# Gate tiles among the merges, merge sums on VectorE, earlier splits of pooled features, recurrence gates one tile later

## The chip, the core and the metric

The kernel runs on one core of a Trainium2 chip. The metric is the device time of one execution in microseconds (us). The core's engines run side by side and wait for each other through semaphores: PE is TensorE's matmul, PEld its weight load, DVE is VectorE, ACT is ScalarE, POOL is GpSimd, SP only issues DMAs. "Clock" is the clock that TensorE was granted as a share of full speed (1.00 is 2.4 GHz, 0.50 is 1.2 GHz).

## What is computed

Two transformer-like models run one after the other on 256 tokens of width 1024, in fp32. Only what the change touches is written out here.

```python
# first block, once
h = rms_norm(x); qa,ka,va,qc,kc,vc,rx,rgate,gates = split(h @ w_in)
ya = moba_attention(qa, ka, va)
xr = causal_dwconv(rx)                          # 4 taps
r = sigmoid(xr @ w_a + b_a); i = sigmoid(xr @ w_x + b_x)   # block-diagonal, 64 wide
yb = scan(exp(-8 r softplus(-lam)), r, i, xr) * gelu(rgate)
yc = rms_norm(diff_attention(qc, kc, vc))
g  = sigmoid(gates + b_gate)                    # 3 x 1024 columns
x  = x + (g0*(ya @ w_branch_a) + g1*(yb @ w_branch_b) + g2*(yc @ w_branch_c)) @ w_out
x  = x + (gelu(conv(rms_norm(x) @ up_g)) * conv(rms_norm(x) @ up_v)) @ ffn_down
x  = rms_norm(x)
# second block, two layers
u,q,k,v,xc,gate_b,gate_c,gate_logits = split(x @ w_in)
oa = (windowed_mean(u) - u) @ w_pool * pool_scale
ob = sliding_window_attention(rope(q), rope(k), v)
oc = gate_b * conv(gate_c * xc)
g  = sigmoid(gate_logits)
x  = layer_norm(a*x + (g0*(oa @ w_branch_a) + g1*(ob @ w_branch_b) + g2*(oc @ w_branch_c)) @ w_o)
x  = layer_norm(a*x + (silu(conv(x @ up_a)) * conv(x @ up_b)) @ w_down)
```

## The kernel before

Everything is held transposed: features on the 128 partitions, the 256 tokens along a row. An fp32 product is made of three matmuls over numbers that are split into a high and a low part: high times high (L332), high weight times low data (L333), low weight times high data (L334). One 128x128 weight tile thus gives three matmuls of 256 columns, and an output tile with eight such weight tiles gives 24.

All weights lie packed in HBM in the order in which they are used. The class `Stream` loads them in chunks of eight tiles (512 KB), and each chunk is split once: ACT copies the high part (`whi`, L175), DVE subtracts for the low part (`wlo`, L176). There are six raw buffers and five pairs of `whi` and `wlo`; `begin` issues the splits of the next chunks a little ahead of the tile that needs them. Each engine works its queue in order; the order comes from a scheduler over the written program.

`phase` runs a list of output tiles: the matmuls of one, its evacuation, and then one step (`fill.slot`) of each attention generator that is live, so that attention work lies between weight tiles. `fill.add` queues generators, `fill.drain` runs them to their end. `reg(i)` hands out one of nine large buffers R0 to R8, `wrk()` one of 13 temporaries of 128x256, `ps()` one of eight PSUM buffers. `split` writes a value's high part with ACT (L344) and its low part with DVE (L345).

The places that the change touches:

- **Recurrence gates.** In the first block tiles of RX and of gate 0 alternate. RX's evacuation is a convolution (L664, L666) and a split into `wrk`; `rg_front(m)` multiplies that split by two block-diagonal weights (6 matmuls) and works out the recurrence's coefficients. `rg_front(m-1)` comes after the gate tile of m, with three tiles between it and its RX tile; `rg_front(7)` comes after the first QC tile, with two. `rg_back` does the scan on DVE.
- **Differential attention's norm.** `diff_norm` turns the four heads' results into `yc` by a reciprocal root on ACT (L460, another activation table than the gates' L763) and a chain on DVE with a split. Three gate tiles follow it, then `rope_tables` (DVE work for the second block, L718 to L731) and the merges.
- **Merges.** One for each of eight output tiles m: three products over the branches (16 weight tiles in the first block, 8 in a layer), each evacuated by DVE with its gate (L859), then two sums and a split into `mg`. Up to m = 5 the sums (L863, L864) and the low part (L872) are POOL's and the high part (L867) and a scaled copy (L871) are ACT's; for m = 6 and 7 the sums and the low part (L869) are DVE's. `late` and `settle` put the split behind the next merge's products. The projection w_out or w_o reads `mg` next, in `seam`: its first three output tiles take k = 0 to 5 of all three first, and k = 6 and 7 after that.
- **Pooled features.** In a layer, two POOL2 tiles are evacuated by a chain of windowed sums (`pool_evac`), and `pool_mix`, after four gate tiles, first splits the two results (L344, L345) and then multiplies them (6 matmuls).

Of the kernel before, what the change touches and what calls it, by code (L numbers as in the profile page):

```python
# [22 lines left out]
NWIN = 6  # L23
POOLAT = 4
# [37 lines left out]
def _plan():  # L62
# [10 lines left out]
    for m in range(8):  # L73
        cols("w_in", 0, RX + m * P)
        cols("w_in", 0, GT + m * P)
        if m:
            runs.append(("rg", 0, 2, m - 1, 1))
    for c in (QC, KC):
        for m in range(4):
            cols("w_in", 0, c + m * P)  # L80
            if c == QC and m == 0:
                runs.append(("rg", 0, 2, 7, 1))
# [3 lines left out]
    for m in range(8, 24):  # L86
        cols("w_in", 0, GT + m * P)
    for m in range(8):
        cols("w_branch_a", 0, m * P, 4)
        cols("w_branch_b", 0, m * P, 8)  # L90
        cols("w_branch_c", 0, m * P, 4)
# [7 lines left out]
    for l in range(2):  # L99
# [10 lines left out]
        for m in range(24):  # L110
            if m == POOLAT:
                runs.append(("pool2", l, 2, 0, 1))
            cols("w_in_2", l, GT2 + m * P)
        for m in range(8):
            cols("w_branch_a_2", l, m * P, 2)
            cols("w_branch_b_2", l, m * P, 4)
            cols("w_branch_c_2", l, m * P, 2)
# [107 lines left out]
def _build(tc, ctx, ap):  # L225
# [549 lines left out]
    for m in range(8):  # L775
        phase([dict(t0=AT["w_in", 0, RX + m * P], nk=8, rhs=HX, evac=rx_evac(m)), gm[m]])
        if m:
            phase([rg_front(m - 1)])
# [61 lines left out]
    phase(gm[:5])  # L840
# [3 lines left out]
    phase(gm[5:])  # L844
    mg = (reg(1, F32R), reg(7, F32R))

    def merge(l, names, nks, srcs, mg):
        def go(m):
# [17 lines left out]
            def parts():  # L866
# [305 lines left out]
```

## Time and profile before

| | |
|---|---|
| median of three runs | 1225.6 us (1219.65 to 1226.5) |
| the profiled execution's own time | 1220.18 us |
| its span, first to last instruction | 1218.4 us |
| mean granted clock | 0.985 |
| PE, DVE, ACT, POOL busy | 1173.7, 948.7, 772.8, 306.7 us |

Busy time counts an engine as busy while an instruction is in flight; matmuls overlap, so PE's busy time hides how far apart they start. The idle time of PE, and the stretches in which matmuls start further apart than elsewhere, are what the rows below are read for.

### The profile page before, as it was taken

How to read it: one execution, taken by the hardware profiler on the slowest of the kernel's cores; microseconds unless marked ns; L12 is line 12 of the kernel's file. 1: busy time of each engine (PE TensorE's matmuls, PEld its weight loads, DVE VectorE, ACT ScalarE, POOL GpSimd, SP SyncE). 2: the span in 40 equal slices, each digit the busy share in tenths (PEclk: the TensorE clock that was granted, in tenths of full speed). 3: DMA queues.
4: the chain of work that ended last, by engine and by line, in shares of the span. 5: the costliest groups of instructions: out<-in, count | busy, mean ns of one | idle time of the engine just before them, and what ended most of it. 6: DMA issues, size and time to landing. Idle time of an engine off the chain costs nothing.

```text
span 1218.4 us, 25304 instructions
## 1 busy us (share of the span) xinstructions
PE 1173.7 (96%) x9928; PEld 1154.2 (95%) x9928; DVE 948.7 (78%) x1713; ACT 772.8 (63%) x1411; POOL 306.7 (25%) x287
## 2 busy tenths in 40 slices
PE   8999999999999999989998999999999998999995
PEld 8998999998999999989998999999999997999995
DVE  7988886788988856876579888757986688987754
ACT  7678566846766645666456766645776556765642
POOL 2033120141132210121155322122320263222122
PEclk9999999999999999989999999999999998999998
DMA  7654545466466655544544466655544553465641
GB/s 285 225 160 138 189 139 175 127 195 202 157 211 196 205 198 179 182 148 156 173 147 152 155 221 196 215 184 170 166 164 158 184 178 124 159 203 184 200 145 35
DMA packets 60487, 212.62 MB, mean 175 GB/s; under 512 B 6864, under 2 KB 9296, under 8 KB 60368
## 3 DMA queue, kind: packets, MB, share of 16 engines
q1 hardware_dynamic: 60080, 210.88, 53.0%
q8 instruction: 77, 1.26, 0.4%
q14 instruction: 42, 0.34, 0.1%
q10 hardware_dynamic: 288, 0.14, 0.1%
HBM read 209.94 MB, written 1.05 MB: 173 GB/s over the span
## 4 chain that ended last, share of the span: by engine, by line
PE 63%; DVE 18%; ACT 8%; POOL 5%; issue 5%; DMA 0%; POOLq 0%; SPq 0%; ACTq 0%; DVEq 0%
PE ps L333 20%; PE ps L332 20%; PE ps L334 20%; DVE wlo L176 7%; ACT whi L175 4%; POOL wrk L925 2%; DVE R L499 1%; POOL wrk L864 1%; DVE wrk L919 1%; DVE wrk L918 1%; PE ps L552 1%; PE ps L749 1%; PE ps L582 1%; PE ps L748 1%; PE ps L750 1%
## 5 line engine op out<-in xcount | busy, mean ns | idle before, releaser
L176 DVE TENSOR_TENSOR wlo<-raw,whi 128x1024 fp32r<-128x1024 f32 (+1 forms) x401 | 501.4, 1254 | 141.6 <-ACT whi L175 136.2
L332 PE MATMUL ps<-hh,whi 128*128 128x256 f32 x1912 | 538.3, 282 | 4.0 <-ACT hh L450 4.0
L333 PE MATMUL ps<-hl,whi 128*128 128x256 f32 x1912 | 534.0, 280 | 3.3 <-DVE hl L451 3.1
L334 PE MATMUL ps<-hh,wlo 128*128 128x256 f32 x1912 | 533.0, 279 | 0.6 <-DVE wlo L176 0.4
L175 ACT CAST whi<-raw 128x1024 fp32r<-128x1024 f32 (+1 forms) x401 | 413.5, 1037 | 149.3 <-PE ps L333 107.4
L332 PEld LDWEIGHTS ps<-hh,whi 128*128 128x128 f32 x1912 | 362.1, 190 | 7.3 <-ACT hh L450 4.6
L333 PEld LDWEIGHTS ps<-hl,whi 128*128 128x128 f32 x1912 | 364.2, 191 | 4.5 <-DVE hl L451 4.0
L334 PEld LDWEIGHTS ps<-hh,wlo 128*128 128x128 f32 x1912 | 362.1, 190 | 1.0 <-DVE wlo L176 1.0
L332 PE MATMUL ps<-R,whi 128*128 128x256 f32 (+1 forms) x1176 | 329.9, 281 | 5.2 <-ACT whi L175 1.9
L333 PE MATMUL ps<-R,whi 128*128 128x256 f32 (+1 forms) x1176 | 329.6, 280 | 5.3 <-DVE R L499 3.0
L334 PE MATMUL ps<-R,wlo 128*128 128x256 f32 (+1 forms) x1176 | 328.5, 279 | 2.6 <-DVE wlo L176 2.6
L333 PEld LDWEIGHTS ps<-R,whi 128*128 128x128 f32 x1176 | 222.6, 189 | 7.8 <-DVE R L499 4.4
L332 PEld LDWEIGHTS ps<-R,whi 128*128 128x128 f32 x1176 | 222.9, 190 | 6.9 <-ACT R L867 2.3
L334 PEld LDWEIGHTS ps<-R,wlo 128*128 128x128 f32 x1176 | 222.5, 189 | 3.4 <-DVE wlo L176 3.4
L925 POOL TENSOR_TENSOR wrk<-wrk 128x256 f32<-128x256 f32 x63 | 82.8, 1315 | 239.7 <-DVE wrk L919 150.3
L344 ACT CAST R<-wrk 128x256 fp32r<-128x256 f32 x89 | 36.0, 407 | 109.5 <-POOL wrk L925 95.2
L918 DVE SCALAR_TENSOR_TENSOR wrk<-ps,par,wrk 128x255 f32<-128x255 f32 x120 | 56.7, 477 | 17.3 <-ACT wrk L917 17.3
L600 POOL TENSOR_SCALAR a_lg<-a_lg,a_r 128x256 f32<-128x256 f32 x24 | 28.8, 1198 | 131.7 <-DVE a_r L575 77.9
L394 POOL TENSOR_TENSOR n_sq<-n_sq,n_q 128x256 f32<-128x256 f32 x42 | 39.6, 942 | 82.4 <-ACT n_q L385 81.2
L345 DVE TENSOR_TENSOR R<-wrk,R 128x256 fp32r<-128x256 f32 x89 | 39.6, 447 | 26.4 <-ACT R L344 26.2
L919 DVE SCALAR_TENSOR_TENSOR wrk<-ps,par,wrk 128x254 f32<-128x254 f32 x120 | 57.2, 477 | 1.6
L863 POOL TENSOR_TENSOR wrk<-wrk 128x256 f32<-128x256 f32 x18 | 17.3, 960 | 137.6 <-DVE wrk L859 137.4
(231 smaller groups left out, 1153.5 us busy)
## 6 DMA issues: line engine op xcount, KB each, us to landing
raw<-in_wst SPq DMA_DIRECT2D x395, 512.0 KB, 3.7
x<-in_xT SPq DMA_DIRECT2D x4, 256.0 KB, 5.1
out_y<-x SPq DMA_DIRECT2D x3, 256.0 KB, 2.2
cst<-in_cst SPq DMA_DIRECT2D x1, 406.0 KB, 8.4
raw<-in_wst SPq DMA_DIRECT2D x1, 384.0 KB, 5.4
par<-in_par SPq DMA_DIRECT2D x1, 312.5 KB, 8.6
raw<-in_wst SPq DMA_DIRECT2D x1, 256.0 KB, 2.6
out_y<-x SPq DMA_DIRECT2D x2, 128.0 KB, 2.0
```

Of the source, the lines that this page charges most:

```text
L175: self.nc.scalar.copy(hi[:, a:b], w[:, a:b])
L176: self.nc.vector.tensor_sub(lo[:, a:b], w[:, a:b], hi[:, a:b].bitcast(F32))
L332: T.matmul(out, sh, mh, start=first, stop=False, skip_group_check=skip)
L333: T.matmul(out, sh, ml, start=False, stop=False, skip_group_check=skip)
L334: T.matmul(out, sl, mh, start=False, stop=last, skip_group_check=skip)
L344: A.copy(hi, src)
L345: V.tensor_sub(lo, src, hi.bitcast(F32))
L394: e.tensor_add(self.sq, self.sq, q)
L600: (G if i else V).tensor_scalar(pe[:, c], pe[:, c], r[:, i:i + 1], None, op0=OP.mult)
L918: V.scalar_tensor_tensor(y[:, 1:], p[:, :S - 1], pr(cw, 44 + i), y[:, 1:], op0=OP.mult, op1=OP.add)
L919: V.scalar_tensor_tensor(y[:, 2:], p[:, :S - 2], pr(cw, i), y[:, 2:], op0=OP.mult, op1=OP.add)
L925: G.tensor_tensor(y, held.pop(j), y, op=OP.mult)
```

## The change

Four edits, and the packing of the weights follows them:

1. `rg_front(m-2)` now comes between RX tile m and gate tile m; `rg_front(6)` and `rg_front(7)` come after the first and the second QC tile; the eight `rg_back` come four and four after the third and fourth QC tile.
2. A merge's two sums and its low part are always DVE's, its high part ACT's (`split` with a scale, L358 and L359 in the new numbering), at once and not behind the next merge.
3. The last gate tiles are done among the merges. First block: gates 0 to 5 of the third branch before the merges, gate 6 after merge 5, gate 7 after merge 6. Layers: the 24 gate tiles go by output tile (three branches of m = 0, then of m = 1, ...); 19 come before the merges, and merges 3 to 7 have one gate tile ahead of each.
4. `pool_evac` splits its result at once into R3 (its sums now stand in R7), and `pool_mix` only multiplies. The four attention generators of a layer are queued before the POOL2 tiles, two tiles earlier.

```diff
+GLEAD, GLEAD2 = 6, 19
+WEAVE = [("merge", m) for m in range(6)] + [("gate", 6), ("merge", 6), ("gate", 7), ("merge", 7)]
+WEAVE2 = [("merge", m) for m in range(3)] + [t for m in range(3, 8) for t in (("gate", GLEAD2 + m - 3), ("merge", m))]
...
-        phase([dict(t0=AT["w_in", 0, RX + m * P], nk=8, rhs=HX, evac=rx_evac(m)), gm[m]])
-        if m:
-            phase([rg_front(m - 1)])
+        phase([dict(t0=AT["w_in", 0, RX + m * P], nk=8, rhs=HX, evac=rx_evac(m))])
+        if m > 1:
+            phase([rg_front(m - 2)])
+        phase([gm[m]])
...
-    phase([qm[0], rg_front(7)])
+    phase([qm[0], rg_front(6), qm[1], rg_front(7)])
     A.activation(rg_q, rg_q, AF.Sqrt, scale=-0.25)
-    for i in range(3):
-        phase([qm[1 + i]])
-        for b in range(3 * i, min(8, 3 * i + 3)):
+    for i in range(2):
+        phase([qm[2 + i]])
+        for b in range(4 * i, 4 * i + 4):
             rg_back(b)
...
-            settle()
-            e = V if m > 5 else G
-            e.tensor_add(g[0], g[0], g[1])
-            e.tensor_add(g[0], g[0], g[2])
...
-                A.activation(mg[0][:, m], g[0], AF.Copy, scale=0.5)
-                if m > 5:
-                    V.scalar_tensor_tensor(mg[1][:, m], g[0], 0.5, mg[0][:, m].bitcast(F32), op0=OP.mult, op1=OP.subtract)
-                else:
-                    A.activation(g[1], g[0], AF.Copy, scale=0.5)
-                    G.tensor_sub(mg[1][:, m], g[1], mg[0][:, m].bitcast(F32))
-            late.append(parts)
-        for m in range(8):
-            go(m)
-        settle()
+            V.tensor_add(g[0], g[0], g[1])
+            V.tensor_add(g[0], g[0], g[2])
+            split(mg[0][:, m], mg[1][:, m], g[0], 0.5)
+        for kind, m in order:
+            if kind == "gate":
+                phase([gm[m]])
+            else:
+                go(m)
...
-            pooled[m] = s
+            pooled[m] = hl2[:, 2 * m], hl2[:, 2 * m + 1]
+            split(*pooled[m], s)
...
-        ab = [(wrk(dt=F32R), wrk(dt=F32R)) for m in range(2)]
-        for m in range(2):
-            split(*ab[m], pooled[m])
...
-        sums = reg(3)
-        phase([dict(t0=w(POOL2, m), nk=8, rhs=HX, evac=pool_evac(m, sums)) for m in range(2)])
+        sums, parts = reg(7), reg(3, F32R)
         fill.gap = 4
         fill.add(*[heads(j) for j in range(4)])
+        phase([dict(t0=w(POOL2, m), nk=8, rhs=HX, evac=pool_evac(m, sums, parts)) for m in range(2)])
```

The order of instructions moves at three places that the prediction speaks of. First, DVE's queue around `pool_mix` of the first layer, before: `R_6932` holds the pooled sums, and the row that reads it is the low part that `pool_mix` needs.

```order
L176 TENSOR_TENSOR wlo<-raw,whi 128x1024
L345 TENSOR_TENSOR R_6766<-wrk,R_6766 128x256
L176 TENSOR_TENSOR wlo<-raw,whi 128x1024 x2
L345 TENSOR_TENSOR wrk<-R_6932,wrk 128x256
L176 TENSOR_TENSOR wlo<-raw,whi 128x1024
```

Of the change, where `R_6926` holds the sums and `R_6927` the parts:

```order
L987 TENSOR_TENSOR R_6926<-R_6926,cst 128x16
L989 SCALAR_TENSOR_TENSOR R_6926<-R_6926,cst,wrk 128x240
L988 TENSOR_TENSOR R_6926<-R_6926,wrk 128x16
L356 TENSOR_TENSOR R_6760<-wrk,R_6760 128x256
L187 TENSOR_TENSOR wlo<-raw,whi 128x1024
L356 TENSOR_TENSOR R_6927<-R_6926,R_6927 128x256
```

The split of the second pooled tile has moved from behind the splits of four weight chunks to the end of its own chain of sums; the first tile's stands a further 21 rows ahead.

Second, DVE's queue at the last merges of the first layer, before, where L859 is the evacuation with the gates (R_7141, R_7558, R_7927 are the three gate buffers):

```order
L859 SCALAR_TENSOR_TENSOR wrk<-R_7141,ps 128x256
L859 SCALAR_TENSOR_TENSOR wrk<-R_7558,ps 128x256
L859 SCALAR_TENSOR_TENSOR wrk<-R_7927,ps 128x256
L176 TENSOR_TENSOR wlo<-raw,whi 128x1024
L859 SCALAR_TENSOR_TENSOR wrk<-R_7141,ps 128x256
```

Of the change, one merge and the gate tile beside it:

```order
L359 SCALAR_TENSOR_TENSOR R_8042<-wrk,R_8041 128x256
L871 SCALAR_TENSOR_TENSOR wrk<-R_7140,ps 128x256
L871 SCALAR_TENSOR_TENSOR wrk<-R_7141,ps 128x256
L873 TENSOR_TENSOR wrk<-wrk 128x256
L871 SCALAR_TENSOR_TENSOR wrk<-R_7142,ps 128x256
L187 TENSOR_TENSOR wlo<-raw,whi 128x1024
L874 TENSOR_TENSOR wrk<-wrk 128x256
L187 TENSOR_TENSOR wlo<-raw,whi 128x1024
```

DVE now has two sums and a low part (L873, L874, L359) in each merge, and a second weight chunk for the gate tile.

Third, DVE's queue at the first merges of the first block, before, where L719 to L725 are `rope_tables`:

```order
L176 TENSOR_TENSOR wlo<-raw,whi 128x1024
L719 TENSOR_SCALAR wrk<-wrk,cst 128x256
L176 TENSOR_TENSOR wlo<-raw,whi 128x1024
L722 TENSOR_SCALAR wrk<-wrk 128x256
L859 SCALAR_TENSOR_TENSOR wrk<-R_663,ps 128x256
L723 TENSOR_SCALAR wrk<-wrk 128x256
L859 SCALAR_TENSOR_TENSOR wrk<-R_2489,ps 128x256
L725 SCALAR_TENSOR_TENSOR wrk<-wrk 128x256
L859 SCALAR_TENSOR_TENSOR wrk<-R_2866,ps 128x256
L725 SCALAR_TENSOR_TENSOR wrk<-wrk 128x256
L176 TENSOR_TENSOR wlo<-raw,whi 128x1024
```

Of the change, with the same work at L733 to L736:

```order
L187 TENSOR_TENSOR wlo<-raw,whi 128x1024
L733 TENSOR_SCALAR wrk<-wrk 128x256
L871 SCALAR_TENSOR_TENSOR wrk<-R_663,ps 128x256
L734 TENSOR_SCALAR wrk<-wrk 128x256
L871 SCALAR_TENSOR_TENSOR wrk<-R_2489,ps 128x256
L736 SCALAR_TENSOR_TENSOR wrk<-wrk 128x256
L871 SCALAR_TENSOR_TENSOR wrk<-R_2866,ps 128x256
L736 SCALAR_TENSOR_TENSOR wrk<-wrk 128x256
L873 TENSOR_TENSOR wrk<-wrk 128x256
L736 SCALAR_TENSOR_TENSOR wrk<-wrk 128x256
L874 TENSOR_TENSOR wrk<-wrk 128x256
```

Before, seven such rows stand between the two chunks' low parts at the rows' end; in the change 23 do here, since thirteen more of the same kinds follow the last row shown before the next `wlo`.

## Rows read from the trace of the kernel before

**Rows 1.** Waits by PE: for what, us in total, times, longest.

```profile
PE ps L333 <- DVE wrk L345: 4.9, 4, 2.1
```

**Rows 2.** Stretches: us, busy (x) of PE, PEld, DVE, ACT, POOL, clock, DMA share, GB/s.

```profile
600.00:624.00 24.00, 24.00 (x215) 24.00 (x213) 15.77 (x25) 10.55 (x18) 15.23 (x15) 1.00 0.46 150
...
103.64:111.55 7.91, 5.52 (x33) 5.13 (x32) 6.65 (x14) 6.93 (x15) 3.64 (x5) 0.78 0.57 162
...
529.00:539.90 10.90, 7.55 (x37) 6.91 (x36) 9.09 (x26) 8.42 (x24) 1.89 (x2) 0.69 0.55 190
533.80:539.90 6.10, 6.05 (x28) 6.05 (x29) 4.29 (x12) 5.64 (x17) 1.89 (x2) 0.50 0.32 128
624.75:632.20 7.45, 4.85 (x26) 4.46 (x26) 6.53 (x16) 3.36 (x7) 2.34 (x3) 0.77 0.42 138
```

**Rows 3.** Timeline of PE at rg_front(7): start, us, line, tile, [idle before, releaser].

```profile
105.41 0.39 PE L332 MATMUL ps<-wrk,whi 128*128 128x256 f32 x1 [1.47 <-ACT wrk L344]
106.72 0.58 PE L333 MATMUL ps<-wrk,whi 128*128 128x256 f32 x1 [0.92 <-DVE wrk L345]
```

**Rows 4.** Timeline of PE at pool_mix, first layer.

```profile
531.14 0.39 PE L333 MATMUL ps<-wrk,whi 128*128 128x256 f32 x1 [1.07 <-DVE wrk L345]
...
533.85 0.58 PE L333 MATMUL ps<-wrk,whi 128*128 128x256 f32 x1 [2.09 <-DVE wrk L345]
```

**Rows 5.** Timeline of DVE at the same place.

```profile
528.40 2.35 DVE L176 TENSOR_TENSOR wlo<-raw,whi 128x1024 fp32r<-128x1024 f32 x2
...
531.01 1.21 DVE L176 TENSOR_TENSOR wlo<-raw,whi 128x1024 fp32r<-128x1024 f32 x1
...
533.38 0.41 DVE L345 TENSOR_TENSOR wrk<-R,wrk 128x256 fp32r<-128x256 f32 x1
```

**Rows 6.** Timeline of PE where w_o follows the first layer's merges.

```profile
626.93 0.39 PE L332 MATMUL ps<-R,whi 128*128 128x256 f32 x1 [1.86 <-ACT R L867]
628.05 0.39 PE L333 MATMUL ps<-R,whi 128*128 128x256 f32 x1 [0.74 <-POOL R L872]
```

**Rows 7.** Timeline of POOL in the first layer's merges, one of them.

```profile
612.12 0.74 POOL L863 TENSOR_TENSOR wrk<-wrk 128x256 f32<-128x256 f32 x1
612.94 1.60 POOL L864 TENSOR_TENSOR wrk<-wrk 128x256 f32<-128x256 f32 x1
615.38 0.75 POOL L872 TENSOR_TENSOR R<-wrk,R 128x256 fp32r<-128x256 f32 x1 [0.84 <-ACT wrk L871]
```

**Rows 8.** Timeline of PE at pool_mix, second layer.

```profile
896.83 0.30 PE L332 MATMUL ps<-wrk,whi 128*128 128x256 f32 x1
897.96 0.39 PE L333 MATMUL ps<-wrk,whi 128*128 128x256 f32 x1 [0.83 <-DVE wrk L345]
```

**Rows 9.** Timelines of PE in the first block's merges.

```profile
228.86 0.38 PE L334 MATMUL ps<-R,wlo 128*128 128x256 f32 x1 [0.97 <-DVE wlo L176]
...
256.09 0.38 PE L334 MATMUL ps<-R,wlo 128*128 128x256 f32 x1 [1.17 <-DVE wlo L176]
...
277.25 0.39 PE L333 MATMUL ps<-R,whi 128*128 128x256 f32 x1 [0.64 <-DVE R L869]
```

**Rows 10.** Timeline of ACT at diff_norm, one head and one gate tile.

```profile
222.58 1.28 ACT L763 ACT_TABLE_LOAD   x1
...
224.37 1.28 ACT L460 ACT_TABLE_LOAD   x1
225.66 0.42 ACT L460 ACTIVATE wrk<-R 128x256 f32<-128x256 f32 x1
```

**Rows 11.** Timeline of DVE beside POOL's sums, first block.

```profile
254.38 3.32 DVE L176 TENSOR_TENSOR wlo<-raw,whi 128x1024 fp32r<-128x1024 f32 x2
```

**Rows 12.** Timeline of DVE at the first block's last merge.

```profile
275.29 0.42 DVE L864 TENSOR_TENSOR wrk<-wrk 128x256 f32<-128x256 f32 x1
275.64 1.22 DVE L176 TENSOR_TENSOR wlo<-raw,whi 128x1024 fp32r<-128x1024 f32 x1
276.77 0.42 DVE L869 SCALAR_TENSOR_TENSOR R<-wrk,R 128x256 fp32r<-128x256 f32 x1
```

More of the change, by code (lines that the diff above doesn't have):

```diff
@@ L80, in _plan @@
             cols("w_in", 0, c + m * P)
-            if c == QC and m == 0:
-                runs.append(("rg", 0, 2, 7, 1))
+            if c == QC and m < 2:
+                runs.append(("rg", 0, 2, 6 + m, 1))
     cols("w_in", 0, VC, 8, 4)
@@ L85, in _plan @@
         cols("w_in", 0, RGT + m * P)
-    for m in range(8, 24):
+    for m in range(8, 16 + GLEAD):
         cols("w_in", 0, GT + m * P)
-    for m in range(8):
-        cols("w_branch_a", 0, m * P, 4)
-        cols("w_branch_b", 0, m * P, 8)
-        cols("w_branch_c", 0, m * P, 4)
+    for kind, m in WEAVE:
+        if kind == "gate":
+            cols("w_in", 0, GT + (16 + m) * P)
+        else:
+            cols("w_branch_a", 0, m * P, 4)
+            cols("w_branch_b", 0, m * P, 8)
+            cols("w_branch_c", 0, m * P, 4)
     for m in range(8):
@@ L109, in _plan @@
                 cols("w_in_2", l, c + m * P)
-        for m in range(24):
-            if m == POOLAT:
+        for n in range(GLEAD2):
+            if n == POOLAT:
                 runs.append(("pool2", l, 2, 0, 1))
[L113 to L117, printed above, removed]
+            cols("w_in_2", l, GT2 + (n % 3 * 8 + n // 3) * P)
+        for kind, m in WEAVE2:
+            if kind == "gate":
+                cols("w_in_2", l, GT2 + (m % 3 * 8 + m // 3) * P)
+            else:
+                cols("w_branch_a_2", l, m * P, 2)
+                cols("w_branch_b_2", l, m * P, 4)
+                cols("w_branch_c_2", l, m * P, 2)
         for m in range(8):
@@ L839, in _build @@
     gm = gates("w_in", 0, GT, 2, hb_g)
-    phase(gm[:5])
+    phase(gm[:GLEAD - 1])
     fill.drain()
@@ L843, in _build, with merge @@
     diff_norm()
-    phase(gm[5:])
+    phase(gm[GLEAD - 1:GLEAD])
     mg = (reg(1, F32R), reg(7, F32R))
-    def merge(l, names, nks, srcs, mg):
+    def merge(l, names, nks, srcs, mg, order, gm):
         def go(m):
@@ L860, in go @@
                 g.append(a)
[L861 to L876 removed]
+            V.tensor_add(g[0], g[0], g[1])
+            V.tensor_add(g[0], g[0], g[2])
+            split(mg[0][:, m], mg[1][:, m], g[0], 0.5)
+        for kind, m in order:
+            if kind == "gate":
+                phase([gm[m]])
+            else:
+                go(m)
     rope_tables()
[L879 removed]
+    merge(0, ("w_branch_a", "w_branch_b", "w_branch_c"), (4, 8, 4), (ya, yb, yc), mg, WEAVE, gm)
     def add_x(m, p):
@@ L1039, in layer @@
         phase(more)
-        sums = reg(3)
-        phase([dict(t0=w(POOL2, m), nk=8, rhs=HX, evac=pool_evac(m, sums)) for m in range(2)])
+        sums, parts = reg(7), reg(3, F32R)
         fill.gap = 4
         fill.add(*[heads(j) for j in range(4)])
+        phase([dict(t0=w(POOL2, m), nk=8, rhs=HX, evac=pool_evac(m, sums, parts)) for m in range(2)])
         phase([dict(t0=w(GC2, m), nk=8, rhs=HX, evac=gc_evac(l, m, xcr, gbr, oc)) for m in range(2)])
-        for i in range(3):
-            gate[i] = reg(4 + i)
-            gm = gates("w_in_2", l, GT2, i, None)
-            if i == 0:
-                phase(gm[:POOLAT])
-                pool_mix(l, oa)
-                gm = gm[POOLAT:]
-            phase(gm)
+        gate[:] = [reg(4 + i) for i in range(3)]
+        gs = [gates("w_in_2", l, GT2, i, None) for i in range(3)]
+        gm = [gs[n % 3][n // 3] for n in range(24)]
+        phase(gm[:POOLAT])
+        pool_mix(l, oa)
+        phase(gm[POOLAT:GLEAD2])
         fill.drain()
         mg = (reg(7, F32R), reg(1, F32R))
-        merge(l, ("w_branch_a_2", "w_branch_b_2", "w_branch_c_2"), (2, 4, 2), (oa, ob, oc), mg)
+        merge(l, ("w_branch_a_2", "w_branch_b_2", "w_branch_c_2"), (2, 4, 2), (oa, ob, oc), mg, WEAVE2, gm)
         ffn_regs(range(5))
```

10 lines of the change are left out of this document (4 added, 6 removed).

## Prediction

> **What bounds the kernel now.** First the busy times in the table: PE is busy 1173.7 of 1218.4 us, the next engine, DVE, 948.7. So PE's matmuls are the bound, and only two things can be won: time in which PE stands still, and time in which its matmuls start further apart. For the first I read PE's waits, of which those for a low part in `wrk` are the largest, 4.9 us in four [rows 1]; for the second the stretches. Where nothing is late, 215 matmuls take 24.00 us at clock 1.00 [rows 2], 0.112 us each, so an output tile of 24 costs 2.7 us. In three stretches that the change touches they are slower. At `rg_front(7)` 7.91 us pass at clock 0.78, at the first layer's `pool_mix` 10.90 us at 0.69, at the end of the first layer's merges 7.45 us at 0.77 [rows 2]. In each PE waits two times or more for a low or high part, and then its clock stands at 0.50 for a while: 6.10 us at `pool_mix` [rows 2]. The loss there is the waits and, on top, the half-speed matmuls behind them.
>
> **The recurrence gates.** PE takes the first matmul of `rg_front(7)` 1.47 us late because ACT's copy of the high part comes late, and the second 0.92 us late because of DVE's subtraction [rows 3]. All other `rg_front` have three tiles between them and their RX tile, this one two. By the code 31 matmuls lie in the stretch (6 of `rg_front`, 24 of the next tile, 1 before), worth 31 x 0.112 = 3.5 us; it took 7.91, so 4.4 are lost. The change puts one tile more, 2.7 us, ahead of it, and the waits sum to 2.4: they go, and the clock's fall with them, I take 4.4. If the clock fell all the same, only 2.4. What is late next: `rg_back` (all DVE) now comes four and four and later, so the weights' low parts behind it come later, and each RX split holds its three of the 13 `wrk` for a tile longer, for which a tanh of ACT can have to wait on POOL. The trace shows neither; bounds 0 and the 0.9 us by which DVE was late here [rows 3]; I take 0.5, the middle, as a new wait.
>
> **The pooled features, layer 1 of 2.** PE waits 1.07 and 2.09 us for the two low parts [rows 4]. DVE wasn't idle: the first part stood behind two chunks' `wlo` (2.35 us), the second behind one more (1.21 us) and a head's softmax [rows 5]. In the change each split follows its sums, before those chunks, as the order shows. By the code 30 matmuls and six short transposes lie in the stretch; 30 x 0.112 is 3.35, the transposes and the start of the small group some 0.8 as in the second layer, where the same passage takes little more than its wait. 10.90 - 4.2 = 6.7 us lost. I take all of it; without the clock it is 3.2. Not free: the attention heads begin two tiles earlier, and the order puts 29 short DVE rows (softmax, sums) between two chunks' low parts. At 0.35 us each, as from 275.29 to 275.64 [rows 12], they are 10 us, less for narrow ones, against five pairs of chunks, four ahead of PE being 4 x 2.7 = 10.7 us. I take 0 and keep 0 to 2 us of wait in each layer.
>
> **The pooled features, layer 2.** One wait of 0.83 us, the next matmul starting 1.13 us after the last instead of 0.11: 1.0 us [rows 8]. No half clock follows. I take 1.0; bounds 0.8 and 1.0.
>
> **The merges, layers.** POOL takes 0.74 + 1.60 us for the two sums, waits 0.84 for ACT and takes 0.75 for the low part [rows 7]: 3.93 us a merge, in step, while PE needs 2.7. So POOL falls behind by 1.2 us in each of six merges, and w_o, which starts with the k of the first merges, stands 1.86 us for ACT's high part of a late one and 0.74 for POOL's low part [rows 6]. The stretch held 26 matmuls, 2.9 us, and took 7.45: 4.5 lost, of which 2.6 are the waits. In the change DVE does three evacuations, two sums, a low part and a chunk's `wlo`. Neighbouring DVE starts are 0.35 us apart for 128x256 and 1.13 us for `wlo` [rows 12], so a merge is 6 x 0.35 + 1.13 = 3.2 us against PE's 2.7. That is behind by 0.5 in merges 0 to 2; from then on each merge has a gate tile beside it, 2 x 2.7 = 5.4 for PE and 3.2 + 1.13 = 4.4 for DVE, so it catches up. The last part comes some 3 us after the last merge's matmuls, and w_o's k = 6 and 7 come 54 matmuls, 6.0 us, after them. I take the 4.5. In the second layer no wait of this kind stood out, 0.
>
> **The merges, first block.** Waits of 0.97, 1.17 and 0.64 us [rows 9], 2.8 together, no half clock. Two are for `wlo`: one where ACT alternates two tables, 1.28 us a load, for `diff_norm` and the gates [rows 10], one where two `wlo` took 3.32 us beside POOL's sums [rows 11] instead of 2 x 1.22 [rows 12]; the third is for a merge's low part. POOL's sums go, so these go. But gates 6 and 7 were the cover of `diff_norm`'s chain, and they move behind it. In the order the third product of merge 0 is now taken head by head, among the next two merges' products, so that PE has work; but 23 DVE rows (rope and two merges) stand between two low parts. 23 x 0.35 = 8.0 us against two chunks ahead, 5.4: 2.6 us of new wait. Removed 2.8, new 2.6: I take +0.2. Bounds: +2.8 if the new wait is hidden, -3 if a head's chain (one load and 1.28 + 0.42 us of ACT [rows 10], and its split) also shows and merges 0 to 2 have nothing left to fill it.
>
> **Sum.** 4.4 - 0.5 + 6.7 + 1.0 + 4.5 + 0.2 = 16.3 us. The profiled execution took 1220.2, so 1203.9; the median of the runs shown is 1225.6, with two of the three there and one at 1219.65, so on that scale 1209.3. I predict 1207.
>
> **A rule on the clock.** The stretches show 0.50 [rows 2] after waits none of which is above 2.09 us, while the waits of up to 1.17 us in the first merges [rows 9] are followed by none. The Trainium skill (TensorE: Matmul & The Clock Gate, HAM oscillation) ties a fall to one long gap in which the engine is idle, and the same page (A second HAM failure mode) also names many short ones. By the first reading these falls aren't due to these waits and stay, which is the first rival's time; by the second they go.
>
> **The rivals.**
>
> *Only the waits go.* The clock falls at these places for another reason, or falls elsewhere instead. Then the terms are 2.4 - 0.5 + 3.2 + 0.8 + 2.6 + 0.2 = 8.7 us: 1211.5 to 1216.9, say 1214. For it: a wait of 1.17 us had no fall. Against it: all three falls follow directly on waits that sum to over 2 us. Chance 0.18.
>
> *The change doesn't do what it says in the layers.* The splits stand early in the queue, but the heads' earlier start makes weights late there instead (the 29 rows, 2 us in each layer, with a fall of the clock in one, 3.4 as at the first `pool_mix`). 16.3 - 4 - 3.4 = 9: about 1214 again. For it: the 10 us estimated against 10.7. Against it: many of those rows are narrow. Chance 0.10.
>
> *DVE becomes the bound of the merges; slower.* In a layer the merges and gates hold 48 short DVE rows and 13 chunks against PE's 13 x 2.7 = 34.9 us. At 0.35 and 1.13 DVE needs 31.5. It decides at a pitch t of 0.42 (48t + 14.7 = 34.9); beyond it each stage loses 48(t - 0.42), three stages 144(t - 0.42), since the first block has the same 48 rows and rope besides. If they ran as slow as `wlo` did beside POOL [rows 11], 3.32 / 2.44 = 1.36 times slower, t is 0.48 and the chunks 1.54: 48 x 0.48 + 13 x 1.54 = 43 a layer, 8 too many, three times 24 us. The merges' 4.5 go too: 1220.2 - (16.3 - 4.5) + 24 = 1232. Against it: what made them slow was POOL, which now stands idle there. Chance 0.04. That half of this, 12 us, with the first block at -3 instead of +0.2 leaves about 1 us of gain, I give 0.08: 1219 to 1224.5 on the two scales, 1222.
>
> *VectorE flushed between instructions.* If neighbouring short rows started 0.42 apart, which is their own duration [rows 12], and chunks 1.22, a layer's merges need 48 x 0.42 + 13 x 1.22 = 36.0 against 34.9: 1.1 us lost in each layer and some 2 in the first block, 1211 instead of 1207. Chance 0.05; in the trace the next starts 0.35 after a row of 0.42 [rows 12]. The Trainium skill has this as a rule (VectorE: DVE Perf Modes, The DRAIN you can't avoid): the next operation doesn't start until the pipe is empty; that row disagrees.
>
> **How the numbers follow.** The forecast holds 0.55; its own range is 1202 to 1211 (the 4 us of wait in the layers on the one side, the first block's +2.8 on the other). The upper end of the whole takes in the first two rivals, 1217 on the median's scale, with 1 for scatter: 1218. The lower end is every term at its best, 4.4 + 6.7 + 1.0 + 4.5 + 2.8 = 19.4 from 1220.2: 1201, with 1 for the scatter of runs: 1200. A measurement of this kernel can tell about 0.5%, 6 us, from no change, as its own three runs lie 7 apart: below 1219.5 is faster. Forecast, both rivals at 1214 and the one at 1211 lie there, 0.88; I leave 0.84, since two of them are near it. Same 0.11, slower 0.05.
>
> **What would show it.** After: no wait of PE for a split part at `rg_front(7)` and `pool_mix`, clock 1.00 over both and at w_o's first matmuls; POOL empty in the merges, DVE rows there 0.35 apart; in the first block PE's waits for `wlo` near 1 us beside rope. It is wrong if the clock's half stretches reappear next to new waits, above all in the first block's merges, or if DVE has no idle time in the merges.

## The result and the profile after

The changed kernel takes 1212.61 us (median of 18 runs, 1203.98 to 1221.05), the kernel before 1225.89 us (18 runs, 1217.93 to 1233.36). The ratio is 0.9895, 95% interval 0.9872 to 0.9919: 13 us faster, within 10 to 16. The forecast was 1207, its own range 1202 to 1211, the range of the whole 1200 to 1218. The profiled execution took 1208.3 us at a span of 1206.3.

The page of the changed kernel (part 1 and the clock line of part 2), and PE's waits (for what, us in total, times, longest) with the rows that are new or were looked for. L343 to L345 are the three matmuls of a product now, L355 and L356 the split, L187 the chunk's low part, L759 to L761 the VC tokens, L563 an attention head's scores.

```profile
PE 1165.5 (97%) x9928; PEld 1146.3 (95%) x9928; DVE 956.2 (79%) x1767; ACT 763.7 (63%) x1391; POOL 245.0 (20%) x233
...
PEclk9999999999999999999999999999999998999898
```

```profile
PE ps L760 <- DVE wlo L187: 2.0, 1, 2.0
...
PE ps L563 <- ACT R L774: 0.8, 1, 0.8
...
PE ps L345 <- DVE wlo L187: 0.7, 2, 0.4
...
PE ps L343 <- DVE a_tl L356: 0.5, 1, 0.5
```

No row speaks of a part in `wrk` from L355 or L356 any more: the four waits of [rows 1] are gone, with those of [rows 3, 4, 8]. POOL has 54 instructions less, which are the merges' three in 18 merges. The stretches of the changed kernel at the same places show the clock (columns as in [rows 2]):

```profile
100.00:112.00 12.00, 11.64 (x103) 11.29 (x101) 10.37 (x19) 10.94 (x25) 5.44 (x7) 1.00 0.52 162
510.00:540.00 30.00, 28.74 (x257) 28.05 (x256) 26.70 (x80) 23.06 (x62) 6.66 (x6) 1.00 0.51 153
600.00:624.00 24.00, 24.00 (x214) 24.00 (x213) 17.80 (x33) 11.22 (x18) 0.52 (x1) 1.00 0.59 193
```

All three are at 1.00 where [rows 2] have 0.78, 0.69 and 0.77. In the last one, the merges and their gate tiles, PE has no idle time, POOL has one short instruction, and DVE has 6.2 us to spare in 24. The timeline of DVE there:

```profile
604.83 0.42 DVE L871 SCALAR_TENSOR_TENSOR wrk<-R,ps 128x256 f32<-128x256 f32 x1
605.16 1.22 DVE L187 TENSOR_TENSOR wlo<-raw,whi 128x1024 fp32r<-128x1024 f32 x1
606.29 0.42 DVE L874 TENSOR_TENSOR wrk<-wrk 128x256 f32<-128x256 f32 x1
607.67 1.23 DVE L187 TENSOR_TENSOR wlo<-raw,whi 128x1024 fp32r<-128x1024 f32 x1 [0.95 <-ACT whi L186]
```

Starts lie 0.33 us apart for a short row and 1.13 for a chunk, as in [rows 12], and DVE waits for ACT, not PE for DVE.

Elsewhere the clock did not rise. The changed kernel's profile has half clock for 3.4 us at 171.3 us and again at 642.3 us, where neither profile of the kernel before has any; it lacks the 3.4 us that the first of those has at 297.5 us. The mean granted clock of its profiled execution is 0.986, against 0.985 in the kernel before.

What came instead of the old waits stands in the VC tokens. PE waits 1.98 us for a chunk's low part, a wait that neither profile of the kernel before has there:

```profile
128.32 0.48 PE L759 MATMUL ps<-whi,hh 128*128 128x512 f32 x1
130.78 0.50 PE L760 MATMUL ps<-wlo,hh 128*128 128x512 f32 x1 [1.98 <-DVE wlo L187]
```

DVE's timeline there (L704 are the recurrence's products, L705 its scans), and ACT's:

```profile
125.66 1.46 DVE L705 TENSOR_TENSOR_SCAN R<-R,R 128x256 f32<-128x256 f32 x2
127.04 0.73 DVE L704 TENSOR_TENSOR R<-R,R 128x256 f32<-128x256 f32 x2
127.69 1.26 DVE L705 TENSOR_TENSOR_SCAN R<-R,R 128x256 f32<-128x256 f32 x2
128.88 0.72 DVE L356 TENSOR_TENSOR R<-ps,R 128x256 fp32r<-128x256 f32 x2
129.52 2.34 DVE L187 TENSOR_TENSOR wlo<-raw,whi 128x1024 fp32r<-128x1024 f32 x2
```

```profile
122.99 1.03 ACT L186 CAST whi<-raw 128x1024 fp32r<-128x1024 f32 x1
...
127.86 0.38 ACT L355 CAST R<-ps 128x256 fp32r<-128x256 f32 x1 [2.62 <-DVE R L704]
```

The wait is DVE's queue. Counted in order, the chunk that PE waits for has its high part from ACT at 122.99, and PE multiplies with it at 128.32; only its low part is late. DVE makes it at 129.52, 5.5 us after the high part was ready, since the eight products, the eight scans, short rows of the heads and two low parts of KC (L356) stand ahead of it; from 119 to 131 us DVE has no gap above 0.08 us.

ACT stands still there too, which looks like the cause and is not. `kc = hi_lo(1, 4)` takes the register that holds the roots `rg_q`, so KC's evacuation on ACT (127.86) waits 2.62 us for the last product (127.04). The chunk whose high part stands behind it on ACT is a later one, and PE doesn't wait for that. In DVE's order as it stands, the register can account for 0.64 us at most, by which KC's low parts stand ahead of the late one; no run shows that share by itself.

To compare kernels place by place I use four marks from the timelines of PE. For the kernel before, in its two profiles (the first, and experiment e12): the end of the VC tokens at 142.0 and 142.4 us; from the last head of the differential attention to the feed-forward norm's statistics (the first block's merges and projection) 84.0 and 83.9 us; from the final norm's statistics to the first layer's (its gates, mixing, merges, projection) 174.8 and 174.6 us; the same of the second layer 170.4 and 170.3 us. The table has the differences to the first profile of before.

| kernel | end of VC tokens | first block's merges | first layer | second layer |
|---|---|---|---|---|
| changed kernel | -0.6 | -2.0 | -10.1 | -1.0 |
| changed kernel again (e11) | -1.0 | -2.0 | -9.5 | -1.0 |
| e1, edit 1 alone | +0.4 | 0.0 | +0.5 | -0.1 |
| e2, edit 4 alone | +0.1 | 0.0 | -3.2 | -1.1 |
| e3, edit 2 alone | -0.2 | -3.1 | -5.6 | -0.7 |
| e7, edit 3 alone | -0.2 | -1.8 | -3.1 | -0.4 |
| e4, all but edit 2 | +0.2 | -1.9 | -8.0 | -1.2 |
| e5, all but edit 1 | +0.3 | -2.4 | -9.9 | -1.3 |
| e6, heads queued later | -0.6 | -0.8 | -11.1 | -2.8 |
| e8, products first | -3.0 | -2.0 | -10.0 | -1.2 |
| e9, e8 and e6, first block unwoven | -3.5 | -2.2 | -11.2 | -2.8 |
| e10, e9 and layers unwoven | -3.3 | -2.7 | -11.0 | -2.1 |
| kernel before again (e12) | +0.3 | 0.0 | -0.2 | -0.1 |

The changed kernel's row sums to 13.7 us, which agrees with the 13 of the medians. That single profiles differ by another amount (12.1 us between the first two spans) has its reason outside these places: the pace and the half clock of the last section. How far a single profile can be trusted is shown by e6, which has the changed kernel's first block unaltered and yet 0.8 us in its merges against 2.0. In the second layer the kernels that queue the heads later (e6, e9, e10) gain 2.1 to 2.8 us, the others with edit 4 1.0 to 1.3. A half-clock stretch of 3.4 us stands at that layer's start in the first profile of before, both of the changed kernel, e1, e2 and e5, and in no other; e4 and e8, which lack it and queue the heads early, still gain only 1.2.

### The profile page after: what moved, and what is told of

It is laid out like the page before. It is cut to its first block, busy times and chain, and to the rows that moved or that the text cites. A ratio compares the mean times of both kernels' runs of the same rounds, so it can differ in the third digit from the quotient of the medians.

```text
span 1206.3 us, 25236 instructions
## 1 busy us (share of the span) xinstructions
PE 1165.5 (97%) x9928; PEld 1146.3 (95%) x9928; DVE 956.2 (79%) x1767; ACT 763.7 (63%) x1391; POOL 245.0 (20%) x233
## 3 DMA queue, kind: packets, MB, share of 16 engines
HBM read 209.94 MB, written 1.05 MB: 175 GB/s over the span
## 4 chain that ended last, share of the span: by engine, by line
PE 65%; DVE 17%; ACT 9%; issue 5%; POOL 3%; DMA 0%; SPq 0%; POOLq 0%; ACTq 0%; DVEq 0%
PE ps L344 20%; PE ps L343 20%; PE ps L345 20%; DVE wlo L187 7%; ACT whi L186 4%; POOL wrk L929 2%; DVE R L510 1%; DVE wrk L923 1%; DVE wrk L922 1%; ACT a_lg L580 1%; PE ps L563 1%; PE ps L760 1%; PE ps L761 1%; PE ps L759 1%; DVE wrk L454 1%
## 5 line engine op out<-in xcount | busy, mean ns | idle before, releaser
L187 DVE TENSOR_TENSOR wlo<-raw,whi 128x1024 fp32r<-128x1024 f32 (+1 forms) x401 | 496.3, 1240 | 118.5 <-ACT whi L186 113.1
L343 PE MATMUL ps<-hh,whi 128*128 128x256 f32 x1912 | 536.5, 281 | 5.1 <-ACT hh L461 3.6
L345 PE MATMUL ps<-hh,wlo 128*128 128x256 f32 x1912 | 531.3, 278 | 0.6 <-DVE wlo L187 0.4
L343 PEld LDWEIGHTS ps<-hh,whi 128*128 128x128 f32 x1912 | 361.6, 189 | 8.3 <-ACT hh L461 4.0
L345 PEld LDWEIGHTS ps<-hh,wlo 128*128 128x128 f32 x1912 | 361.1, 189 | 1.0 <-DVE wlo L187 1.0
L343 PE MATMUL ps<-R,whi 128*128 128x256 f32 (+1 forms) x1180 | 330.2, 281 | 6.8 <-ACT R L355 3.8
L345 PE MATMUL ps<-R,wlo 128*128 128x256 f32 (+1 forms) x1180 | 327.9, 279 | 0.4 <-DVE wlo L187 0.2
L343 PEld LDWEIGHTS ps<-R,whi 128*128 128x128 f32 x1180 | 223.6, 190 | 9.0 <-ACT R L355 4.5
L345 PEld LDWEIGHTS ps<-R,wlo 128*128 128x128 f32 x1180 | 223.1, 189 | 1.3 <-DVE wlo L187 1.2
L929 POOL TENSOR_TENSOR wrk<-wrk 128x256 f32<-128x256 f32 x63 | 82.9, 1316 | 238.6 <-DVE wrk L923 150.3
L355 ACT CAST R<-wrk 128x256 fp32r<-128x256 f32 x89 | 36.0, 407 | 117.5 <-POOL wrk L929 95.3
L356 DVE TENSOR_TENSOR R<-wrk,R 128x256 fp32r<-128x256 f32 x89 | 38.9, 440 | 27.0 <-ACT R L355 26.9
L611 POOL TENSOR_SCALAR a_lg<-a_lg,a_r 128x256 f32<-128x256 f32 x24 | 25.3, 1056 | 113.1 <-DVE a_r L586 60.9
L509 ACT ACTIVATE R<-x,par 128x256 fp32r<-128x256 f32 x48 | 23.8, 507 | 27.8 <-DVE x L889 16.0
```

The source lines that it names most:

```text
L187: self.nc.vector.tensor_sub(lo[:, a:b], w[:, a:b], hi[:, a:b].bitcast(F32))
L343: T.matmul(out, sh, mh, start=first, stop=False, skip_group_check=skip)
L345: T.matmul(out, sl, mh, start=False, stop=last, skip_group_check=skip)
L355: A.copy(hi, src)
L356: V.tensor_sub(lo, src, hi.bitcast(F32))
L611: (G if i else V).tensor_scalar(pe[:, c], pe[:, c], r[:, i:i + 1], None, op0=OP.mult)
```

## The experiments

**One edit at a time.** e1 is the kernel before with `rg_front` and `rg_back` of the change; e2 with its pooled features and the heads queued earlier; e3 with its sums; e4 is the changed kernel with POOL's sums.

```diff
 e3
-            settle()
-            e = V if m > 5 else G
-            e.tensor_add(g[0], g[0], g[1])
-            e.tensor_add(g[0], g[0], g[2])
...
-            late.append(parts)
+            V.tensor_add(g[0], g[0], g[1])
+            V.tensor_add(g[0], g[0], g[2])
+            split(mg[0][:, m], mg[1][:, m], g[0], 0.5)
```

> Only the recurrence gates are moved (edit 1), the rest is as before. Theory, local give-back: the two waits at the last recurrence gate and the half clock behind them go, about 4.4 us are won there, but the eight scans now stand closer together on DVE ahead of a weight chunk, so PE waits about 2 us for that chunk's low part in the VC tokens and 0.9 us at two or three places of the RX tiles; the end of the VC tokens comes about 0.6 us earlier than in the kernel before, the whole time is the same within 2 us. Rival, the wait in the VC tokens comes from another edit: it isn't there, and 3.9 us are won.

Measured: ratio 1.0023 (0.9988 to 1.0058). The theory held in the main, and the give-back is even complete: the VC tokens begin 3.5 us earlier than in the kernel before and end 0.4 later, not 0.6 earlier. The two waits at the RX and QC tiles are 0.37 and 0.34 us, not 0.9. PE's waits of e1 have the row that the kernel before lacks, and a half-clock stretch of 3.4 us follows it:

```profile
PE ps L749 <- DVE wlo L176: 1.9, 1, 1.9
```

> Only the pooled features are split at once and the heads queued two tiles earlier (edit 4). Theory, the waits brought the clock down: both waits in the first layer and the 6.8 us of half clock go, 6.7 us less there, 1.0 in the second layer, less up to 1.3 of new waits beside the heads; the stretch from the first layer's start to its layer norm is 5 to 6 us shorter. Rival, only the waits go: half clock stays near the mixing, 3.2 and 0.8 us won. The merges' wait of 1.86 + 0.74 us and the half clock behind it stay in both.

Measured: 0.9968 (0.9935 to 1.0001). The waits for the parts are gone and the second layer is 1.1 us shorter, as the theory said; but in the first layer only 3.2 us are won, the rival's number. The timeline of PE shows why: two new waits stand 4 us further on, at an attention head's scores, and in this run a half-clock stretch of 3.4 us begins behind them (at 535.9).

```profile
534.14 0.95 PE L552 MATMUL ps<-R,R 64*128 64x128 f32 x11 [0.59 <-ACT R L763]
535.59 0.38 PE L332 MATMUL ps<-hh,whi 128*128 128x256 f32 x1 [0.50 <-DVE a_tl L345]
```

> Only the merges' sums and low parts are DVE's (edit 2); no gate tile lies among the merges. Theory, DVE needs 3.2 us a merge against PE's 2.7 and falls behind by about 4 us over eight merges of a layer, which the 54 matmuls ahead of k = 6 and 7 (6 us) only just cover: the wait for POOL goes, 3 to 4.5 us won in the first layer, perhaps with up to 1 us of wait left. Rival, without the gate tiles the wait only changes its engine: PE waits over 1.5 us for DVE at the projection in the first layer, under 2 us won. First block: the wait of 1.17 us for a low part goes in both, the one of 0.97 stays.

Measured: 0.9974 (0.9940 to 1.0008). The first layer is 5.6 us shorter, more than the theory's 4.5; 1.7 of it can be the mixing's half clock, 3.4 us in this profile and 6.8 in the first of before. The wait at the projection is gone altogether, with the half clock behind it, without any gate tile among the merges: the theory, and DVE's lag is covered. In the first block the wait of 1.17 us is gone, 0.98 stays and one of 0.51 is new; its merges are 3.1 us shorter.

> The whole change, but the merges' sums and low parts up to m = 5 are POOL's as before. Theory, time beside the merges is what counts: with a gate tile in five of eight merges PE needs 5.4 us for each and POOL 3.9, so POOL catches up and no wait is left at the projection of the first layer: there within 1 us of the changed kernel; in the first block DVE's chunk splits are slow beside POOL again, and 1 to 2 us of the gain there are lost. Rival, the engine is what counts: the wait of about 2.6 us and the half clock behind it come back, 4.5 us more than the changed kernel.

Measured: 0.9882 (0.9835 to 0.9930). POOL does catch up; two short waits are left at the projection, without half clock:

```profile
622.08 0.38 PE L343 MATMUL ps<-R,whi 128*128 128x256 f32 x1 [0.23 <-ACT R L879]
623.27 0.39 PE L344 MATMUL ps<-R,whi 128*128 128x256 f32 x1 [0.81 <-DVE R L881]
```

So the layer is 2.1 us longer than in the changed kernel, not within 1 and not 4.5: time beside the merges counts for most of it, the engine for the rest. For the first block the theory missed: it expected 1 to 2 us of the gain there to be lost, and -1.9 us against -2.0 is none.

**What the first results left open.** e5 is the changed kernel without edit 1, e6 queues the heads later, e7 is edit 3 alone, e8 issues the products first.

```diff
 e6
-        fill.gap = 4
-        fill.add(*[heads(j) for j in range(4)])
         phase([dict(t0=w(POOL2, m), nk=8, rhs=HX, evac=pool_evac(m, sums, parts)) for m in range(2)])
+        fill.gap = 4
+        fill.add(*[heads(j) for j in range(4)])
 e8
+    km = [dict(t0=AT["w_in", 0, KC + m * P], nk=8, rhs=HX, evac=to_hi_lo(kc, m)) for m in range(4)]
+    for i, mt in enumerate(qm[2:] + km):
+        phase([mt])
+        if i < 2:
+            for c in range(4 * i, 4 * i + 4):
+                V.tensor_tensor(rg_i[:, c], rg_i[:, c], rg_q[:, c], op=OP.mult)
+        for c in ((), (0, 1), (2, 3), (4, 5), (6,), (7,))[i]:
+            rg_back(c)
```

> The whole change without edit 1: recurrence gates and scans as in the kernel before. Theory, edit 1 gives its gain back: the waits of 1.47 and 0.92 us at the last recurrence gate are there again, the 1.95 us in the VC tokens is not; the end of the VC tokens lies within 1.5 us of the changed kernel, the whole time within 0.3% of it. Rival, edit 1 is worth its 3.9 us: slower than the changed kernel by about 4 us.

Measured: 0.9926 (0.9898 to 0.9955). The waits of 1.46 and 0.92 us are back, the one in the VC tokens is not there, and the tokens end 0.9 us later than in the changed kernel's first profile. So at its place edit 1 is worth about 1 us, not 3.9. The whole times don't decide: the ratio is 0.0031 above the changed kernel's first one, 3.8 us, and 0.0013 above that of e11, and the intervals overlap.

> The whole change, but the four heads of a layer are queued after the POOL2 tiles as before. Theory, the two new waits beside the scores in the first layer (0.77 for ACT's gate, 0.50 for a low part) come from the earlier heads: both go, 1.3 us less there, and the split pooled features still come in time. Rival, they come from the gates' new order: they stay, and no more than 0.3 us changes.

Measured: 0.9898 (0.9865 to 0.9931). Both waits beside the scores are gone, the first layer is 11.1 us shorter than before instead of 10.1, and the pooled features still wait for nothing. The theory held. The whole time doesn't show it (0.9895 for the changed kernel).

> Only the last gate tiles lie among the merges (edit 3); sums on POOL up to m = 5, recurrence gates and pooled features as before. Theory from the traces: POOL (3.9 us a merge) gets 5.4 us in five of eight merges, the wait of 1.86 + 0.74 us at the first layer's projection shrinks to about 1 us without half clock, 3 to 4 us won there, about 1 us in the first block; 4 to 5 us in all, 0.4%. Rival from the median times (the whole change is 13 us, edits 1, 2 and 4 alone come to about 4): weaving alone is worth 8 to 9 us, 0.7%, in places that the profile does not show as waits.

Measured: 0.9971 (0.9939 to 1.0003). That is near the theory's 0.4%, and not clear of no change. The waits at the projection shrink as in e4, and no half clock follows; the rival's 0.7% lies just beyond the interval's end.

```profile
626.54 0.38 PE L341 MATMUL ps<-R,whi 128*128 128x256 f32 x1 [0.25 <-ACT R L876]
627.73 0.38 PE L342 MATMUL ps<-R,whi 128*128 128x256 f32 x1 [0.80 <-DVE R L878]
```

> The whole change, with the recurrence's eight products issued together after the third and fourth QC tile and the scans two by two behind the following tiles, so that the register of the roots, which the KC tiles overwrite, comes free earlier. Theory, the wait of 1.95 us in the VC tokens is a chain: KC's evacuation on ACT waits for the last product, the next chunk's high part stands behind it, and its low part behind the scans: the wait falls under 0.5 us, the end of the VC tokens comes 2 us earlier than in the changed kernel. Rival, DVE is simply full there: the wait moves to a later chunk and the end of the VC tokens stays within 0.5 us.

Measured: 0.9880 (0.9834 to 0.9925). The wait in the VC tokens is gone and they end 2.4 us earlier than in the changed kernel, so the rival is out. It was forecast from a chain over ACT; what the rows show is DVE's order. The chunk's high part is ready at about the same time (124.4 us, in the changed kernel 124.0), and its low part, at 129.52 before, now comes at 126.91, ahead of the last two scans (L704 here) and of KC's later low parts:

```profile
126.31 0.67 DVE L704 TENSOR_TENSOR_SCAN R<-R,R 128x256 f32<-128x256 f32 x1
126.91 1.19 DVE L187 TENSOR_TENSOR wlo<-raw,whi 128x1024 fp32r<-128x1024 f32 x1
128.02 1.26 DVE L704 TENSOR_TENSOR_SCAN R<-R,R 128x256 f32<-128x256 f32 x2
```

One wait of 0.77 us is new, right behind the tokens, for a head's low part.

**Putting them together.** e9 is e8 and e6 in one, with the first block's gate tiles all before the merges; e10 the same for the layers, so that edit 3 is gone and DVE's sums stay.

```diff
-GLEAD, GLEAD2 = 6, 19
-WEAVE = [("merge", m) for m in range(6)] + [("gate", 6), ("merge", 6), ("gate", 7), ("merge", 7)]
-WEAVE2 = [("merge", m) for m in range(3)] + [t for m in range(3, 8) for t in (("gate", GLEAD2 + m - 3), ("merge", m))]
+GLEAD, GLEAD2 = 8, 24
+WEAVE = [("merge", m) for m in range(8)]
+WEAVE2 = [("merge", m) for m in range(8)]
```

> The changed kernel with three alterations that the runs so far point to: the recurrence's products first, the heads queued after the POOL2 tiles, and in the first block all gate tiles before the merges as in the kernel before (the sums stay on DVE). Theory, the local gains add: 2.4 us at the VC tokens, 1.0 in the first layer, 1.1 in the first block's merges, 4 to 4.5 us faster than the changed kernel, about 0.9860 of the kernel before. Rival, they don't add, since a wait that goes at one place comes back at the next seam: the span differs from that of the kernel with products first by less than 0.5 us of waits.

Measured: 1207.34 us, 0.9862 (0.9824 to 0.9900), beside 0.9913 (0.9877 to 0.9950) of the changed kernel on the same chip. The places give 3.5, 2.2, 11.2 and 2.8 us: the local gains add at the tokens and in the first layer; in the first block's merges leaving the gate tiles unwoven is worth 0.2 here and 0.7 in e10, which has the same first block, not 1.1, and e6's 1.2 us of scatter there covers both.

> As the last, and in the layers too all 24 gate tiles come before the merges (by output tile, as in the changed kernel). Theory, DVE's sums alone remove the wait at the projection, so the gate tiles among the merges are not needed: no wait over 0.5 us at w_o's first matmuls, the first layer within 0.5 us of the last kernel. Rival, DVE's lag of 0.5 us a merge shows at the projection: 1 to 2 us of wait there.

Measured: 1204.13 us, 0.9843 (0.9809 to 0.9876), the fastest of all. The first layer is 11.0 us shorter than before, e9's is 11.2, and the projection waits for nothing. The stretch from the merges into the feed-forward norm, of e10 and then of e9:

```profile
590.00:650.00 60.00, 57.47 (x487) 56.30 (x485) 57.90 (x109) 35.65 (x60) 20.05 (x18) 1.00 0.54 169
```

```profile
590.00:650.00 60.00, 57.46 (x487) 56.30 (x487) 51.36 (x87) 34.93 (x60) 20.05 (x18) 1.00 0.54 174
```

DVE is busy 57.9 of 60 us in e10 and 51.4 in e9, and PE does the same 487 matmuls in both. In e10 the merges lie from 590 to 613 us, and a merge takes DVE 3.13 us (low parts end at 607.00, 610.13 and 613.27), close to the 3.2 of the prediction, while PE needs 2.7. So DVE without gate tiles beside the merges is all but full and falls behind, and PE still has no wait over 0.25 us at the projection. e10 is clearly faster than the kernel before; its interval ends where that of the changed kernel beside it begins (0.9876 and 0.9877), so that it beats the changed kernel is likely, not certain.

> The changed kernel once more, unaltered, beside the two others on one chip, and for its profile. Theory, two paces: at full clock the matmuls of whole stretches start 0.1133 or 0.1177 us apart, and which of the two a stretch gets changes from one execution to the next of the same program; the long feed-forward stretches show another pattern than in the first profile of this kernel, and the waits at the touched places are the same within 0.1 us. Rival, the pace belongs to the program: the same pattern as in its first profile.

Measured: 1213.52 us, 0.9913 (0.9877 to 0.9950). The waits at the touched places are as in the first profile (1.95 for 1.98 in the VC tokens). The pace of the feed-forward stretches was also nearly as in the first profile; that part speaks for the rival.

> The kernel before once more, unaltered, for a second profile. Theory, two paces: another pattern of paces over the feed-forward stretches than in its first profile; the waits at the touched places are the same within 0.1 us, and the half-clock stretches behind the waits at the first layer's mixing and projection are there again. Rival, the half clock at those places was chance: at least one of the two is missing.

Measured: 1224.46 us. The waits are there again (1.48 and 0.92 us at the last recurrence gate; 1.08 and 2.10 at the mixing; 1.85 and 0.69 at the projection), and so are the half-clock stretches behind the last two, 3.4 us (at 532.4) and 6.8 us (at 624.6); behind the recurrence gate there was none this time. The pace was another than in the first profile, see below. New against the first profile: 0.96 us for a low part in the last KC tile, ahead of the VC tokens, 1.63 instead of 1.17 us in the first block's merges, and a second wait at the second layer's mixing (0.80 and 0.83 instead of 0.83). So the waits are the same within 0.1 us at the three places of the first list, but not everywhere.

## Why the prediction was right, and where its terms were off

**The whole.** The 13 us (10 to 16) lie below the forecast's 16.3 and above the 8.7 and 9 of the first two rivals. 1212.6 is inside the range of the whole, but above the forecast's own 1202 to 1211, and nearer to 1214 than to 1207; part of that is the scale, on which 1225.6 - 16.3 gave 1209.3. By places, the gates missed by about 3 us and the first layer by 1, and the first block's merges brought 1.8 more than forecast: that the misses partly cancel is luck.

**The recurrence gates: +4.4 - 0.5 predicted, 0.6 to 1.0 measured.** The step that failed is the give-back, "I take 0.5". The gain came: the tokens begin 2.9 to 3.7 us earlier in the profiles with edit 1. They take 2.3 us longer, which is the 1.98 wait and its slow restart; waits of 0.36 and 0.35 us for the evacuations of an RX and a QC tile came too. The mechanism was right, a weight's low part behind the scans on DVE; the size was wrong. Its upper bound of 0.9 us was taken from a wait at another place, and the products and scans ahead of the low part were not added up: they and the short rows among them fill DVE from 120.23 to 128.95 us. e8 shows it by changing that order, e5 by going back.

**The pooled features and merges of the first layer: 6.7 + 4.5 predicted, 9.5 to 10.1 measured.** Both mechanisms held; the term for the earlier heads, taken at 0 with a bound of 2, is the difference: 0.77 + 0.50 us of wait in the changed kernel, which e6 removes. e6, e9 and e10 have 11.0 to 11.2 there, the predicted sum. The gain at the two places holds what the clock gave back there.

**The second layer: 1.0 predicted, 1.0 measured.** The first profile of before and both of the changed kernel have the half clock at the layer's start. Without it, e12 waits 0.80 and 0.83 us at the mixing, and e4 and e8 wait 0.60 and 0.50 us beside the heads. With the heads later the layer gains 2.1 to 2.8. So the change won more than 1.0 here and gave a part back to the earlier heads; that 1.0 is left is in part luck.

**The first block's merges: 0.2 predicted, 2.0 measured.** The new wait was sized too high. Where the 23 rows stand PE waits 0.33 us, for a merge's evacuation by DVE, not 2.6 for a low part; one of 0.65 for a head's high part is new, and those of 0.97, 1.17 and 0.64 went. The term that failed is the cover, "two chunks ahead, 5.4". The 23 rows took 7.2 us (234.07 to 241.23), not 8.0, and PE's first matmul with the late low part comes three chunks, 8.4 us, after the end of the low part before it. The two rows that meet:

```profile
241.23 1.22 DVE L187 TENSOR_TENSOR wlo<-raw,whi 128x1024 fp32r<-128x1024 f32 x1
```

```profile
242.26 0.28 PE L344 MATMUL ps<-R,whi 128*128 128x256 f32 x1
242.50 0.39 PE L345 MATMUL ps<-R,wlo 128*128 128x256 f32 x1
```

The low part ends at 242.44 or 242.45, and the matmul starts 0.24 us after the one ahead of it instead of 0.11: it came just in time.

**The rivals.** *Only the waits go* is out for the three places, where the half clock went with the waits, but not in its second half, that the clock falls elsewhere instead. An estimate of what the clock costs is one minus the granted clock, times the span: in the mean it is 18.2 us over 68 runs of the kernel before and 15.5 over 25 of the changed kernel. That is some 3 us less, where the forecast put 16.3 - 8.7 = 7.6 on the clock. New falls such as those at 171.3 and 642.3 us take back a part, so on the clock the result stands between the forecast and this rival. Of the prediction's two readings of the rule on the clock, the second fits the three places: the falls there went with waits none of which was above 2.1 us. *The change doesn't do what it says* was half right in e2 alone (new waits and a half clock there), and cost 1.3 us of waits in the first layer of the whole change. *DVE becomes the bound* is out: the pitch is 0.33, below the 0.42 from which it would decide, PE waits for no low part over 0.25 us in the merges, and e10 shows how little room is left without the gate tiles. *VectorE flushed between instructions* is out: short rows of 0.42 us start 0.33 apart in the changed kernel too. The Trainium skill (VectorE: DVE Perf Modes, The DRAIN you can't avoid) says that the next operation waits for an empty pipe, and adds, which the prediction left out, that one which isn't held starts earlier; the rows here agree with that addition.

**What carries the gain.** No edit alone gives more than about 0.3%: 1.0023, 0.9974, 0.9971, 0.9968 for edits 1 to 4, and each interval takes in 1. By the places, edits 2 and 3 remove the same wait, each most of it. The medians can't confirm that: the four changes sum to 0.64%, give or take some 0.7%, against 1.05% for the whole. e4, without edit 2, is as fast as the whole within its interval; edit 3 was taken out only together with other alterations, in e10. As far as the places tell, the change's 13 us are the pooled features and either of these, in the first layer, 2 us in the first block, and about 1 us each in the second layer and at the gates.

## What to carry to other kernels

When a block of work is moved later, add up what now stands ahead of the next weights in that engine's own queue, and compare it with how far ahead the weights are made. When a wait has two suspects, follow the very tile that was late: here ACT stood still for 2.6 us beside the wait, but the tile's high part had been ready for 5 us. Two edits that attack one wait don't add, so a change of several parts is best measured in parts; here one of four edits could go and another be taken back in part, together with a new order of the products, and the kernel was at least as fast. In the kernel before, a wait followed by half-speed matmuls cost about twice its length; what is won in the mean is less, since the fall doesn't always come and can come elsewhere.

## What the runs showed of the hardware

**Half clock behind waits.** In the 14 profiles the mixing's wait of 1.1 + 2.1 us was followed by half clock in 5 of 5 (both profiles of before, e1, e3, e7), for 3.4 or 6.8 us; the projection's 1.9 + 0.7 in 4 of 4 (both of before, e1, e2). The recurrence gate's 1.5 + 0.9 was in 4 of 6, the VC tokens' 1.95 in 2 of 5, the first layer's scores' 0.6 to 0.8 + 0.5 in 1 of 6. Where these waits were absent, there was none at these places. Waits that the change leaves alone show chance at work too: the pair in the differential attention (0.6 to 0.8 + 0.6) was followed by half clock in 1 of 14, the changed kernel's first profile, and the pair at the first layer's norm (0.4 + 0.6) in 3 of 14. The same wait in the same kernel can be followed by 3.4 us, 6.8 us or nothing, so a single profile prices it only roughly.

**Two paces at full clock.** At clock 1.00 the matmuls of whole stretches start 0.1133 us apart, or 0.1177, 4% more, and nothing waits. The same stretch of the two profiles of the kernel before, the first and then the second:

```profile
690.00:790.00 100.00, 99.53 (x874) 99.14 (x873) 86.30 (x135) 64.70 (x113) 24.89 (x18) 1.00 0.63 200
```

```profile
690.00:790.00 100.00, 99.87 (x849) 99.67 (x849) 84.81 (x132) 63.64 (x111) 24.11 (x18) 1.00 0.65 197
```

874 matmuls against 849 in the same 100 us. A feed-forward stretch of some 1600 matmuls costs 7 us more at the slower pace; e3, e5 and e6 had it in the first block (e3 stood 3.3 us ahead of the kernel before when that stretch began, and 2.0 behind at its end), e2, e4, e6 and e8 in the first layer's. Part of it can come back: in the last feed-forward stretch PE waits 2.8 us for ACT at the fast pace, and 0.7 at the slow one. This is larger than most terms of the prediction, and fits the 15 us over which the runs of one kernel scatter. What sets the pace stays open: it differs between two executions of one kernel, but the two profiles of the changed kernel agree, and no experiment here changed it on purpose.
